# Attention of a two-layer trunk: V of all heads first through DRAM, q and k of a head as one Strassen product

## The chip, the cores and the metric

The kernel runs on one core of one Trainium2 chip. The metric is the device time of one execution in microseconds (us), lower is better. A core has five engines that run their own queues in order and wait for one another by semaphores: TensorE (PE in the profile; its weight loads are PEld), VectorE (DVE), ScalarE (ACT), GpSimd (POOL) and SyncE (SP). SP issues every DMA of this kernel, so a DMA that has to wait for something holds back all DMAs behind it.

## The reference, cut to what matters

One sequence of 1024 tokens with 1024 channels passes two layers: an HGRN2 mixer with its feed-forward network, then dilated attention with a second feed-forward network, and a last norm. The change touches the attention.

```python
def dilated_attention_mixer(u, w_qkv, w_out, cos, sin):        # u: 1 x 1024 x 1024
    qkv = (u @ w_qkv).reshape(B, S, 3, ATTN_HEADS, ATTN_HEAD_DIM)   # 12 heads of 128
    q = apply_rope(qkv[:, :, 0], cos, sin)
    k = apply_rope(qkv[:, :, 1], cos, sin)
    v = qkv[:, :, 2]
    for gi, (window, dilation) in enumerate(((128, 1), (512, 4), (2048, 16))):
        ...                                    # 4 heads each: softmax(mask(q k^T / sqrt(128))) v
        outs.append(o_g); lses.append(lse_g)
    alpha = jax.nn.softmax(lse, axis=2)        # merges the three groups, token by token
    return (o * alpha[..., None]).reshape(B, S, ATTN_WIDTH) @ w_out
```

## The kernel before

Activations lie transposed: a tile has 128 channels as partitions and the 1024 tokens along the row, in two halves of 512 (`hs(hh)`). Each float32 operand of a large product is split into a high and a low part (`split`, `split_w`: ScalarE casts, VectorE subtracts), and a product is three matmuls: high by high, high by low, low by high. The operands `v` of the attention projections are the eight tiles of the normed input, split. `unit` makes one projection of one head: it loads a 512 KB weight tile, splits it, and issues 8 x 2 x 3 matmuls of 128x512 into two PSUM banks (pool `pmm`, four banks).

The loop over j (0 to 3) and gi (0 to 2, dilations 1, 4 and 16) does one head n = 4 gi + j at a time, so heads come in the order 0, 4, 8, 1, 5, 9 and so on. `attn_scores` makes q and k by `unit` and applies the rotary embedding (`rope`), which also writes the tokens in the order of the dilated residue classes (`tok`); for dilations 4 and 16 that is a strided access. Then it makes eight score blocks of 128 rows (tiles `as`, in the four banks of pool `pax`). For each block VectorE adds the mask and takes the row maximum in one instruction into `st` (L671), then scales the maxima (`ng`, L675), and ScalarE takes the exponentials with their sums (L677). `attn_value` makes v of the head, undoes the norm, and transposes it on TensorE (L691). `attn_out` transposes the probabilities (`apx`, L707), copies them back, and multiplies (`apo`, L715). When the three heads of one j have their scores, `attn_weights` sends maxima and sums through DRAM to bring them into token order (`dn`, `cm`), computes the merge weights, and sends these through DRAM (`dw`); `attn_merge` loads each broadcast over partitions (`wb`) and multiplies it into the head's output (L763). After the loop the twelve outputs are split (`aov`), and `mixer_out` multiplies by the output weights (`p_n3..`, two parts of six heads per output tile) and adds the residual. In the second part of a layer, `ffn_in` already uses a two-by-two Strassen form.

The program is recorded in this order, and a scheduler then sets the order of each engine's queue once, before it runs; on the chip each queue is strictly in that order. Buffers come from pools of tags with a fixed number of tiles: `wr` (raw weights) 2, `wh` and `wl` (split weights) 3 each, `wx` 2, `ws` 4, `vc` 8, `va` 16, `vb` 12, each 128 x 1024.

Of the kernel before, what the change touches and what calls it, by code (L numbers as in the profile page):

```python
# [40 lines left out]
def trunk_kernel(ctx, tc, x, cols, consts, w_in, w_hout, w_qkv, w_aout, w_ffn, w_down, out):  # L41
# [588 lines left out]
    def rope(ps, dil, name):  # L630
        t = big("vc", name)
        bb = big("wx", f"{name}b")
        for hh in range(2):
# [4 lines left out]
            nc.vector.tensor_add(tv, tv, nat(bb[:, hs(hh)], dil))
        return t

    def attn_scores(j, gi, st):
# [36 lines left out]
        return blocks, place  # L678

    def attn_value(j, gi):  # L680
        dil = (1, 4, 16)[gi]
# [1 line left out]
        pv = unit(w_qkv[2 * NH + n], v, f"av{n}")
        vt = big("wx", f"avt{n}")
        for hh in range(2):
            nc.vector.tensor_mul(tok(vt, dil, hh), nat(pv[hh][:], dil), nat(rb[:, hs(hh)], dil))
# [208 lines left out]
```

## Time and profile before

| | |
|---|---|
| median of 3 runs | 2608.99 us (2608.29 to 2609.2) |
| span of the profiled execution | 2605.1 us |
| busy, share of the span | PE 98%, PEld 81%, DVE 66%, ACT 30%, POOL 5% |
| attention stage, from the last matmul of the first layer | 1274 us to about 1807 us |

The time of a run is that of the device, some 4 us more than the span from the first to the last instruction of the program. A matmul's end is modelled in the trace, and matmuls overlap, so the work of TensorE is better counted in issue slots than in busy time.

### The profile page before, as it was taken

To read this page: it belongs to the slowest core of one execution; us is meant where nothing else is said; L and a number is where in the kernel's file an instruction comes from. 1 tells how busy PE (TensorE), PEld (TensorE's weight loads), DVE (VectorE), ACT (ScalarE), POOL (GpSimd) and SP (SyncE) were. 2 spreads that over 40 slices of the span, in tenths; PEclk is the share of its full clock that TensorE was granted. 3 is DMA by queue.
4 is the path that set the end of the run, shared out by engine and by line. 5 is a ranking of instruction groups with operands and counts; after the bars stand their busy time and mean duration, and the time that the engine had idled before them with its cause. 6 is when DMAs were issued, how large, how long until landed. Compare 5 with 4: busy or idle time off the path is not lost.

```text
span 2605.1 us, 30351 instructions
## 1 busy us (share of the span) xinstructions
PE 2546.4 (98%) x12044; PEld 2118.4 (81%) x12044; DVE 1732.1 (66%) x2957; ACT 785.1 (30%) x1168; POOL 129.9 (5%) x107
## 2 busy tenths in 40 slices
PE   8999999999999999999999999999999999999998
PEld 6888888788888888888887878787878888888887
DVE  8888888977777777433545464636377777775336
ACT  5222222344323233212231313134242323333212
POOL 1111111111000000000000000000010000000000
PEclk9999999999999999999999999999999999999999
DMA  3101111142222224531211121213322222236323
GB/s 144 33 33 33 33 33 33 44 143 89 79 84 80 89 81 149 183 100 61 97 41 58 41 58 41 61 34 101 115 81 89 81 89 81 81 102 229 110 58 127
DMA packets 77518, 215.24 MB, mean 83 GB/s; under 512 B 21696, under 2 KB 24000, under 8 KB 77376
## 3 DMA queue, kind: packets, MB, share of 16 engines
q1 hardware_dynamic: 77376, 213.30, 25.3%
q8 instruction: 95, 1.56, 0.2%
q14 instruction: 47, 0.39, 0.0%
HBM read 173.28 MB, written 39.99 MB: 82 GB/s over the span
## 4 chain that ended last, share of the span: by engine, by line
PE 81%; DVE 11%; DMA 3%; issue 2%; ACT 1%; POOL 1%; SPq 0%; POOLq 0%; DVEq 0%; ACTq 0%
PE pt L483 6%; PE pt L482 6%; PE pt L481 6%; PE pfw L125 6%; PE pfw L127 6%; PE pfw L124 6%; PE pb L482 4%; PE pb L483 4%; PE pb L481 4%; PE p_n L125 2%; PE p_n L124 2%; PE p_n L127 2%; PE lv L327 2%; PE as L670 1%; PE p_aq L127 1%
## 5 line engine op out<-in xcount | busy, mean ns | idle before, releaser
L563 DVE TENSOR_TENSOR h<-pfw,h 128x512 f32<-128x512 f32 (+1 forms) x104 | 63.6, 646 | 217.6 <-PE pfw L127 217.5
L108 ACT CAST h_fw<-r_fw 128x896 fp32r<-128x896 f32 (+1 forms) x60 | 58.3, 973 | 249.7 <-PE pfw L125 206.4
L108 ACT CAST h_fa<-r_fg 128x1024 fp32r<-128x1024 f32 x44 | 46.4, 1056 | 198.4 <-PE pt L482 183.5
L108 ACT CAST h_fb<-s 128x1024 fp32r<-128x1024 f32 x44 | 46.4, 1054 | 171.1 <-PE pb L482 159.6
L342 DVE COPY_PREDICATED at<-lm,lv 128x192 f32<-128x192 uint8 (+2 forms) x288 | 82.2, 353 | 4.0 <-PE lv L327 3.2
L677 ACT ACTIVATE ap<-ap,ng 128x256 f32<-128x256 f32 (+1 forms) x96 | 41.9, 438 | 124.4 <-DVE ng L675 124.4
L156 POOL TENSOR_TENSOR rs_n<-ms_n,half 128x8 f32<-128x8 f32 (+2 forms) x7 | 9.0, 1281 | 1353.8 <-DVE ms_n L154 1353.8
L494 DVE TENSOR_TENSOR s<-r_fu 128x512 f32<-128x512 f32 x44 | 30.3, 691 | 65.8 <-DMA r_fu<-in_w_ffn_dram 65.7
L482 PE MATMUL pb<-n3b,h_fa 128*128 128x512 f32 x176 | 68.7, 390 | 2.6 <-DVE n3b L456 2.6
L109 DVE TENSOR_TENSOR l_fw<-r_fw,h_fw 128x896 fp32r<-128x896 f32 (+1 forms) x60 | 67.1, 1121 | 4.6 <-ACT h_fw L108 4.0
L482 PE MATMUL pb<-n1b,h_fa 128*128 128x512 f32 x176 | 68.6, 390 | 1.2 <-DVE n1b L456 1.2
L481 PE MATMUL pb<-n3b,h_fa 128*128 128x512 f32 x176 | 68.8, 391 | 0.5 <-ACT n3b L455 0.5
L481 PE MATMUL pt<-n3t,h_fb 128*128 128x512 f32 x176 | 68.6, 390 | 0.0
L481 PE MATMUL pt<-n1t,h_fb 128*128 128x512 f32 x176 | 68.6, 390 | 0.0
L481 PE MATMUL pb<-n1b,h_fa 128*128 128x512 f32 x176 | 68.6, 390 | 0.0
L483 PE MATMUL pb<-n3b,l_fa 128*128 128x512 f32 x176 | 68.5, 389 | 0.0
L482 PE MATMUL pt<-n3t,h_fb 128*128 128x512 f32 x176 | 68.5, 389 | 0.0
L483 PE MATMUL pb<-n1b,l_fa 128*128 128x512 f32 x176 | 68.5, 389 | 0.0
L483 PE MATMUL pt<-n1t,l_fb 128*128 128x512 f32 x176 | 68.5, 389 | 0.0
L483 PE MATMUL pt<-n3t,l_fb 128*128 128x512 f32 x176 | 68.5, 389 | 0.0
L482 PE MATMUL pt<-n1t,h_fb 128*128 128x512 f32 x176 | 68.5, 389 | 0.0
L517 DVE TENSOR_TENSOR t<-pt,t 128x512 f32<-128x512 f32 x44 | 30.4, 691 | 51.0 <-PE pt L483 50.9
(1036 smaller groups left out, 7840.3 us busy)
## 6 DMA issues: line engine op xcount, KB each, us to landing
r_fu<-in_w_ffn_dram SPq DMA_DIRECT2D x44, 512.0 KB, 3.6
r_fg<-in_w_ffn_dram SPq DMA_DIRECT2D x44, 512.0 KB, 3.6
act<-g SPq DMA_DIRECT2D x44, 512.0 KB, 2.6
st<-act SPq DMA_DIRECT2D x44, 512.0 KB, 4.3
r_fw<-in_w_down_dram SPq DMA_DIRECT2D x44, 448.0 KB, 3.4
h<-hd SPq DMA_DIRECT2D x16, 512.0 KB, 5.5
r_fw<-in_w_down_dram SPq DMA_DIRECT2D x16, 512.0 KB, 3.6
r_aq<-in_w_qkv_dram SPq DMA_DIRECT2D x12, 512.0 KB, 3.6
```

Source lines behind the costliest of these rows:

```text
L108: nc.scalar.copy(hi[:, a:b], src[:, a:b])
L109: nc.vector.tensor_sub(lo[:, a:b], src[:, a:b], hi[:, a:b].bitcast(F32))
L124: nc.tensor.matmul(p[:, 0:b - a], wh, vh[:, a:b], start=(first and i == 0), stop=False)
L125: nc.tensor.matmul(p[:, 0:b - a], wh, vl[:, a:b], start=False, stop=False)
L127: nc.tensor.matmul(p[:, 0:b - a], wl, vh[:, a:b], start=False, stop=(last and i == n - 1))
L327: nc.tensor.matmul(ps[:, c * 192:c * 192 + 192], kk[:, hh * 512 + c4 * P:hh * 512 + c4 * P + P], mb[:, c4 * 192:c4 * 192 + 192], start=Tru ...
L342: nc.vector.copy_predicated(av[:, :, d:4, :], mk[:, :, d:4, :], pv[:, :, s0:s0 + 4 - d, :])
L481: nc.tensor.matmul(ps[:], wh, bh, start=(kk == 0), stop=False)
L482: nc.tensor.matmul(ps[:], wh, bl, start=False, stop=False)
L483: nc.tensor.matmul(ps[:], wl, bh, start=False, stop=(kk == 3))
L563: nc.vector.tensor_add(h[d][:, a:b], ps[i][:, 0:b - a], h[d][:, a:b])
L677: nc.scalar.activation(place[b], place[b], AF.Exp, bias=ng[:, b:b + 1], scale=SCALE, accum_out=st[:, gi, b, 1:2])
```

## The change

V is made first, for four heads at once and by tokens: the input is the stationary operand, the weights of four heads (512 columns) are the moving one, and each block of 128 tokens is scaled by the norm, and written to a DRAM tile `vd`. A head later reads its v from there in the order of its dilation, so that no transpose of v is left. The operands are then the blocks b11, b12, b21, b22 of the input, two by two in channels and tokens, and four combinations t1 to t4.

q and k of a head are one product of two-by-two blocks with seven block products instead of eight (`pair`). Each is 12 matmuls; I call them a to g by the weight tiles a to g: a is b11, b is t1, c is t2, d is b21, e is t3, f is b22 and g is t4. Sums are made by accumulating onto a PSUM bank that ScalarE has seeded by a copy: p2 from p1 before c, p3 from p2 before e. q of the first half is ready after d (p1), k of the second after e (p3 and s5), q of the second after f (p2 and s5), and k of the first after g, which accumulates onto p3 once more. `rope` now takes one half at a time: ScalarE copies the two halves of 64 rows into `z`, crossed, VectorE multiplies by sine and cosine and adds. There is one `z` per head, so the four calls of a head follow one another. For the two halves with s5, VectorE first adds s5 in the strided order, and ScalarE then reads that strided tile.

The projections of the next head are recorded ahead of the scores of this one. The probabilities are transposed back into their own tile. Each head's output goes to a DRAM tile `od`, and the merge of all twelve heads (load `am`, load `wb`, multiply, split) stands after the last head.

```diff
@@ -598,25 +598,138 @@
...
+    def halves(w, src, scale=None):
+        hi, lo = w[:, 0:512], w[:, 512:T]
+        if scale is None:
+            nc.scalar.copy(hi, src)
+            nc.vector.tensor_sub(lo, src, hi.bitcast(F32))
+        else:
+            nc.scalar.activation(hi, src, AF.Copy, scale=scale)
+            nc.vector.scalar_tensor_tensor(lo, src, scale, hi.bitcast(F32), ALU.mult, ALU.subtract)
+        return w
 
     def done0(h, d, lo, hi, i):
         nm.add(h[d], d)
         nc.sync.dma_start(hd[1][d], h[d][:])
-        v[d] = split(h[d], "va", f"v2_{d}", gain(2, d))
-
-    ffn_down(0, act0, hd[0], done0)
-    nm.begin()
-    done_ps["aq0"] = unit(w_qkv[0], v, "aq0")
+        for hh in range(2):
+            halves(qops[d % 4][f"b{d // 4 + 1}{hh + 1}"], h[d][:, hs(hh)], gain(2, d))
+
+    h = ffn_down(0, act0, hd[0], done0)
+
+    vd = dp.tile([T, NH * P], F32, name="vd")
+    wn = [0]
+
+    def v_weights(g):
+        ws = []
+        for kp in range(4):
+            raw = big("wr", f"vr{g}_{kp}")
+            for b in range(2):
+                kb = 2 * kp + b
+                src = raw[:, hs(b)]
...
+                w = big(("wh", "wl", "ws")[wn[0] % 3], f"vw{g}_{kb}", F32R)
+                wn[0] += 1
+                ws.append(halves(w, src))
+        return ws
+
+    for g in range(3):
+        ws = v_weights(g)
+        for tt in range(8):
+            ps = mmps(f"pv{g}_{tt}")
+            for kb in range(8):
+                op = qops[kb % 4][f"b{kb // 4 + 1}{tt // 4 + 1}"]
+                o = tt % 4 * P
+                vh, vl = op[:, o:o + P], op[:, 512 + o:512 + o + P]
+                wh, wl = ws[kb][:, 0:512], ws[kb][:, 512:T]
+                nc.tensor.matmul(ps[:], vh, wh, start=(kb == 0), stop=False)
+                nc.tensor.matmul(ps[:], vh, wl, start=False, stop=False)
+                nc.tensor.matmul(ps[:], vl, wh, start=False, stop=(kb == 7))
+            if g == 0 and tt == 0:
+                nm.begin()
+            if tt % 2 == 0:
+                vs = big("wx", f"vs{g}_{tt}")
+            nc.scalar.activation(vs[:, hs(tt % 2)], ps[:], AF.Copy, scale=nm.r[:, tt:tt + 1])
+            nc.sync.dma_start(vd[cs(tt), g * 512:g * 512 + 512], vs[:, hs(tt % 2)])
+
...
+            nc.vector.tensor_sub(dst, x1, x0)
+            qops[kk][n] = halves(big("va" if n == "t4" else "vb", f"q{n}_{kk}", F32R), dst)
+
...
+    def w_half(src, name):
+        wn[0] += 1
+        return halves(big(("wh", "wl")[wn[0] % 2], name, F32R), src)
+
+    def pair_weights(ga, up, name):
+        g0, g1, u0, u1 = ga[:, hs(0)], ga[:, hs(1)], up[:, hs(0)], up[:, hs(1)]
+        w = {"b11": w_half(g0, f"{name}a")}
+        nc.vector.tensor_sub(g0, g0, u0)
+        nc.vector.tensor_add(u0, u0, u1)
+        w["t1"] = w_half(u0, f"{name}b")
+        nc.vector.tensor_sub(u0, u1, g0)
+        w["t2"] = w_half(u0, f"{name}c")
+        w["b21"] = w_half(g1, f"{name}d")
+        nc.vector.tensor_sub(g1, g1, u0)
+        w["t3"] = w_half(g0, f"{name}e")
+        w["b22"] = w_half(g1, f"{name}f")
+        w["t4"] = w_half(u1, f"{name}g")
+        return w
+
+    def seeded(ps, w, ops, n, onto=True):
+        for kk in range(4):
+            wh, wl = w[n][:, cs(kk)], w[n][:, 512 + kk * P:512 + kk * P + P]
+            bh, bl = ops[kk][n][:, 0:512], ops[kk][n][:, 512:T]
+            nc.tensor.matmul(ps[:], wh, bh, start=(kk == 0 and not onto), stop=False, skip_group_check=onto)
+            nc.tensor.matmul(ps[:], wh, bl, start=False, stop=False, skip_group_check=onto)
+            nc.tensor.matmul(ps[:], wl, bh, start=False, stop=(kk == 3), skip_group_check=onto)
+
+    def pair(ga, up, ops, s5, name):
+        w = pair_weights(ga, up, name)
+        p1, p5, p2, p3 = [mmps(f"{n}_{name}") for n in ("p1", "p5", "p2", "p3")]
+        seeded(p1, w, ops, "b11", False)
+        nc.scalar.copy(p2[:], p1[:])
+        seeded(p5, w, ops, "t1", False)
+        nc.scalar.copy(s5, p5[:])
+        seeded(p2, w, ops, "t2")
+        nc.scalar.copy(p3[:], p2[:])
+        seeded(p1, w, ops, "b21")
+        yield p1
+        seeded(p3, w, ops, "t3")
+        yield p3
+        seeded(p2, w, ops, "b22")
+        yield p2
+        seeded(p3, w, ops, "t4")
+        yield p3
...
+    def rope(t, ps, s5, hh, dil, z):
+        tv = tok(t, dil, hh)
+        src, zn = nat(ps[:], dil), nat(z, dil)
+        if s5 is not None:
+            nc.vector.tensor_add(tv, src, nat(s5, dil))
+            src = tv
+        nc.scalar.copy(zn[0:64], src[64:128])
+        nc.scalar.copy(zn[64:128], src[0:64])
+        nc.vector.tensor_mul(z, z, sb[:, hs(hh)])
+        nc.vector.tensor_mul(tv, src, nat(cb[:, hs(hh)], dil))
+        nc.vector.tensor_add(tv, tv, zn)
+
+    def attn_qk(j, gi):
         dil = (1, 4, 16)[gi]
         n = gi * 4 + j
...
+        ga = load_raw(w_qkv[n], D, f"aq{n}")
+        up = load_raw(w_qkv[NH + n], D, f"ak{n}")
+        sz = big("wx", f"sz{n}")
+        s5, z = sz[:, 0:512], sz[:, 512:T]
+        p = pair(ga, up, qops, s5, f"a{n}")
+        q = big("vc", f"aq{n}")
+        k = big("vc", f"ak{n}")
+        rope(q, next(p), None, 0, dil, z)
+        rope(k, next(p), s5, 1, dil, z)
+        rope(q, next(p), s5, 1, dil, z)
+        rope(k, next(p), None, 0, dil, z)
+        return q, k
+
+    def attn_scores(j, gi, st, q, k):
+        n = gi * 4 + j
         blocks = []
...
+    od = dp.tile([NH, P, T], F32, name="od")
+
+    def attn_out(j, gi, vv, blocks, ptiles):
...
+        for ti, (t, where) in enumerate(ptiles):
+            for g1 in range(0, len(where), 4):
+                grp = where[g1:g1 + 4]
+                ps = axps(f"apx{n}_{ti}_{g1}")
+                for c, key in enumerate(grp):
+                    pts[key] = t[:, cs(g1 + c)]
+                    nc.tensor.transpose(ps[:, cs(c)], pts[key], ident)
                 nc.scalar.copy(t[:, g1 * P:(g1 + len(grp)) * P], ps[:, 0:len(grp) * P])
...
-        return o
+        nc.sync.dma_start(od[n], o[:])
...
-    def attn_merge(j, dw, os3):
-        for gi in range(3):
-            wb = big("ws", f"wb{j}_{gi}")
-            nc.sync.dma_start(wb[:], dw[gi].partition_broadcast(P))
-            nc.vector.tensor_mul(os3[gi][:], os3[gi][:], wb[:])
...
+    heads = [(j, gi) for j in range(4) for gi in range(3)]
+    dws = []
+    qk = {heads[0]: attn_qk(*heads[0])}
+    for i, (j, gi) in enumerate(heads):
+        if i + 1 < NH:
+            qk[heads[i + 1]] = attn_qk(*heads[i + 1])
+        if gi == 0:
+            st = sp.tile([P, 3, 8, 2], F32, tag="st", name=f"st{j}", bufs=2)
+        blocks, ptiles = attn_scores(j, gi, st, *qk.pop((j, gi)))
+        if gi == 2:
+            dws.append(attn_weights(j, st))
+        vv = attn_value(j, gi)
+        attn_out(j, gi, vv, blocks, ptiles)
+    ov = []
+    for i, (j, gi) in enumerate(heads):
+        o = big("vc", f"am{j}_{gi}")
+        nc.sync.dma_start(o[:], od[gi * 4 + j])
+        wb = big("wx", f"wb{j}_{gi}")
+        nc.sync.dma_start(wb[:], dws[j][gi].partition_broadcast(P))
+        nc.vector.tensor_mul(o[:], o[:], wb[:])
+        ov.append(split(o, "va" if i < 8 else "vb", f"aov{i}"))
```

How the queues change is seen in three places. Names end in buffer numbers; the digit before it is the head (`ak4` is k of head 4, `as0` a score block of head 0, `a8e` the weights e of head 8, `st0` the statistics of j = 0).

The first is VectorE's queue where a head's rotary embedding meets the scores. Before, k of head 4 is finished and then its own scores are reduced:

```order
L637 TENSOR_TENSOR ak4_10196<-p_ak4_0_10146,cb_9842 128x128x4
L634 TENSOR_TENSOR ak4b_10197<-p_ak4_1_10147,sb_9843 64x512
L638 TENSOR_TENSOR ak4_10196<-ak4_10196,ak4b_10197 128x128x4
L635 TENSOR_TENSOR ak4b_10197<-p_ak4_1_10147,sb_9843 64x512
L637 TENSOR_TENSOR ak4_10196<-p_ak4_1_10147,cb_9842 128x128x4
L109 TENSOR_TENSOR l_ak8_10417<-r_ak8_10414,h_ak8_10416 128x1024
L638 TENSOR_TENSOR ak4_10196<-ak4_10196,ak4b_10197 128x128x4
L671 ISA ap4_0_10206,st0_9848<-as4_1_10209,kon_96 128x256
L671 ISA st0_9848 128x1
L671 ISA ap4_0_10206,st0_9848<-as4_5_10214,kon_96 128x256
```

In the change:

```order
L751 TENSOR_TENSOR sz4_10800<-sz4_10800,sb_10644 128x512
L752 TENSOR_TENSOR ak4_10802<-ak4_10802,cb_10643 128x128x4
L747 TENSOR_TENSOR aq4_10801<-p2_a4_10830,sz4_10800 128x128x4
L753 TENSOR_TENSOR ak4_10802<-ak4_10802,sz4_10800 128x128x4
L612 TENSOR_TENSOR a8e_11043<-r_aq8_11020,a8e_11043 128x512
L799 ISA ap0_0_10942,st0_10941<-as0_1_10945,kon_96 128x256
L799 ISA st0_10941 128x1
L799 ISA ap0_0_10942,st0_10941<-as0_3_10950,kon_96 128x256
L799 ISA st0_10941 128x1
L751 TENSOR_TENSOR sz4_10800<-sz4_10800,sb_10644 128x512
L752 TENSOR_TENSOR aq4_10801<-aq4_10801,cb_10643 128x128x4
L799 ISA ap0_0_10942,st0_10941<-as0_1_10945,kon_96 128x256
```

The reductions of head 0 now stand between the steps of the rotary embedding of head 4, behind an addition that needs p2 of head 4, and the rest of head 4 stands behind them; the scores of head 4 come one head later.

The second is VectorE's queue at the merge weights of a j (`cm` is what comes back from DRAM). Before, for j = 1:

```order
L686 TENSOR_TENSOR avt9_11436<-p_av9_1_11387,rb_n2_9829 128x32x16
L109 TENSOR_TENSOR l_av2_11656<-r_av2_11653,h_av2_11655 128x1024
L741 TENSOR_TENSOR amx1_11365<-cm1_11363 128x8
L742 TENSOR_TENSOR amx1_11365<-amx1_11365,cm1_11363 128x8
L745 TENSOR_TENSOR ae1_11368<-cm1_11363,amx1_11365 128x24
L749 TENSOR_TENSOR ale1_11371<-ae1_11368,cm1_11363 128x24
L751 TENSOR_TENSOR ad1_11373<-ale1_11371 128x8
L752 TENSOR_TENSOR ad1_11373<-ad1_11373,ale1_11371 128x8
L753 RECIPROCAL ad1_11373<-ad1_11373 128x8
L754 TENSOR_TENSOR ae1_11368<-ae1_11368,ad1_11373 128x24
L763 TENSOR_TENSOR ao1_10877<-ao1_10877,wb1_0_11479 128x1024
L634 TENSOR_TENSOR aq2b_11546<-p_aq2_0_11495,sb_9843 64x512
```

In the change, for j = 0:

```order
L803 TENSOR_SCALAR ng8_11383<-st0_10941 128x8
L612 TENSOR_TENSOR a9a_11694<-r_aq9_11687,a9a_11694 128x512
L694 TENSOR_TENSOR r_aq9_11687<-r_aq9_11687,r_ak9_11689 128x512
L695 TENSOR_TENSOR r_ak9_11689<-r_ak9_11689 128x512
L870 TENSOR_TENSOR amx0_11419<-cm0_11417 128x8
L871 TENSOR_TENSOR amx0_11419<-amx0_11419,cm0_11417 128x8
L874 TENSOR_TENSOR ae0_11422<-cm0_11417,amx0_11419 128x24
L612 TENSOR_TENSOR a9b_11699<-r_ak9_11689,a9b_11699 128x512
L878 TENSOR_TENSOR ale0_11425<-ae0_11422,cm0_11417 128x24
L697 TENSOR_TENSOR r_ak9_11689<-r_ak9_11689,r_aq9_11687 128x512
L880 TENSOR_TENSOR ad0_11427<-ale0_11425 128x8
L751 TENSOR_TENSOR sz5_11467<-sz5_11467,sb_10644 128x512
```

The merge itself (L763) is gone from here. The first instruction that reads `cm` now stands ahead of the weights b of head 9 and of the first rotary step of head 5.

The third is SP's queue at the end of the attention. Before, when the last statistics (`dn3`) are sent:

```order
L72 DMA r_n3w4_1_13336<-in_w_aout_dram 128x768
L733 DMA dn3_13053<-st3_12336 512x1x2 x2
L584 DMA n3h0_13233<-hd1_4571 128x1024
L72 DMA r_n3w1_0_13456<-in_w_aout_dram 128x768
L738 DMA cm3_13059<-dn3_13053 128x48
L72 DMA r_fu1_0_14019<-in_w_ffn_dram 128x1024
L72 DMA r_fu1_1_14295<-in_w_ffn_dram 128x1024
L72 DMA r_n3w1_1_13462<-in_w_aout_dram 128x768
L756 DMA dw3_13074<-ae3_13064 128x3x8
L762 DMA wb3_0_13175<-dw3_13074 128x1024
L762 DMA wb3_1_13178<-dw3_13074 128x1024
L762 DMA wb3_2_13181<-dw3_13074 128x1024
```

In the change:

```order
L851 DMA od_10650<-ao7_13202 128x1024
L862 DMA dn3_13267<-st3_12942 512x1x2 x2
L904 DMA am0_0_13319<-od_10650 128x1024
L867 DMA cm3_13273<-dn3_13267 128x48
L851 DMA od_10650<-ao11_13293 128x1024
L904 DMA am0_1_13328<-od_10650 128x1024
L904 DMA am0_2_13337<-od_10650 128x1024
L906 DMA wb0_2_13339<-dw0_11432 128x1024
L904 DMA am1_0_13346<-od_10650 128x1024
L885 DMA dw3_13288<-ae3_13278 128x3x8
L906 DMA wb1_0_13348<-dw1_12099 128x1024
L904 DMA am1_1_13355<-od_10650 128x1024
```

Before, three `wb` loads are left behind the last statistics. Now twelve loads of head outputs and ten of `wb` stand behind them (the two others, for heads 0 and 4, a little ahead), each `wb` into one of two tiles of `wx`; 12 of these 24 rows are shown. On TensorE the transposes of the probabilities of a head now stand between the matmuls c of the head that comes two places later (those of head 0 between `a8c`), and its `apo` matmuls among the matmuls d there.

## Rows read from the trace of the kernel before

**Rows 1.** The page: span, and busy time of each engine.
```profile
span 2605.1 us, 30351 instructions
...
PE 2546.4 (98%) x12044; PEld 2118.4 (81%) x12044; DVE 1732.1 (66%) x2957; ACT 785.1 (30%) x1168; POOL 129.9 (5%) x107
```

**Rows 2.** Windows: stretch, length, busy time (x instructions), clock, DMA share, GB/s.
```profile
640.00:1000.00 360.00, 360.00 (x1590) 298.20 (x1589) 277.70 (x340) 109.64 (x132) 0.00 (x0) 1.00 0.25 84
1274.00:1807.00 533.00, 512.28 (x2546) 423.71 (x2544) 284.71 (x518) 147.10 (x337) 1.64 (x1) 1.00 0.19 54
...
1808.00:1812.00 4.00, 3.35 (x9) 2.62 (x10) 4.00 (x4) 1.95 (x3) 0.00 (x0) 0.64 0.03 8
```

**Rows 3.** The windows of the output projection's matmuls (tile p_n) alone, TensorE.
```profile
1274.00:1807.00 533.00, 19.91 (x83) 1.00 0.19 54
```

**Rows 4.** Waits of TensorE from 1265 to 1830: total, times, longest.
```profile
PE as L670 <- DVE ak L638: 16.5, 11, 1.8
```

**Rows 5.** The chain that ended last: start, us, what.
```profile
1277.70 1.78 PE nm_n L181 x16
...
1304.58 2.31 PE as L670 x10
...
1315.53 1.64 PE apx L707 x15
1317.16 3.35 PE apo L715 x30
```

**Rows 6.** Groups by form: busy us, mean ns | idle before. V's transposes, VectorE.
```profile
L691 PE MATMUL avp<-kon,avt 128*128 128x128 f32 x96 | 14.6, 282 | 2.9 <-DVE avt L686 2.6
...
L671 DVE CUSTOM_DVE_ANT_0 ap<-as,kon 128x256 f32<-128x256 f32 x44 | 18.1, 422 | 4.4 <-PE as L670 3.7
...
L638 DVE TENSOR_TENSOR aq<-aq,aq4b 128x512 f32<-128x512 f32 x2 | 2.2, 1096 | 0.0
...
L638 DVE TENSOR_TENSOR ak<-ak,ak0b 128x512 f32<-128x512 f32 x2 | 1.4, 690 | 0.0
...
L109 DVE TENSOR_TENSOR l_fd<-r_fu,h_fd 128x512 fp32r<-128x512 f32 x19 | 12.9, 681 | 0.0
```

**Rows 7.** The same of ScalarE.
```profile
L677 ACT ACTIVATE ap<-ap,ng 128x256 f32<-128x256 f32 x44 | 21.8, 497 | 89.7 <-DVE ng L675 89.7
L721 ACT COPY ao<-apo 128x512 f32<-128x512 f32 x16 | 16.7, 1070 | 5.9 <-PE apo L715 5.9
...
L717 ACT COPY ao<-apo 128x512 f32<-128x512 f32 x8 | 4.7, 586 | 7.9 <-PE apo L715 7.9
```

**Rows 8.** Timeline of head 9 (dilation 16): VectorE: start, length.
```profile
1503.80 1.08 DVE L637 TENSOR_TENSOR aq<-p_aq,cb 128x512 f32<-128x512 f32 x1
...
1525.28 0.17 DVE L675 TENSOR_SCALAR ng<-st 128x8 f32<-128x8 f32 x1
```

**Rows 9.** Timeline of ScalarE at the exponentials of head 0.
```profile
1309.37 0.49 ACT L677 ACTIVATE ap<-ap,ng 128x256 f32<-128x256 f32 x1
...
1309.86 0.50 ACT L677 ACTIVATE ap<-ap,ng 128x256 f32<-128x256 f32 x1
```

**Rows 10.** Timeline of the last merge, from statistics to output matmuls.
```profile
1787.47 1.21 SPq L733 DMA_DIRECT2D dn<-st  x2
...
1794.05 0.33 SPq L738 DMA_DIRECT2D cm<-dn  x1
...
1797.27 0.17 DVE L741 TENSOR_TENSOR amx<-cm 128x8 f32<-128x8 f32 x1 [2.06 <-DMA cm<-dn]
...
1802.28 1.28 SPq L762 DMA_DIRECT2D wb<-dw  x3
1806.24 2.53 DVE L763 TENSOR_TENSOR ao<-ao,wb 128x1024 f32<-128x1024 f32 x2 [6.51 <-DMA wb<-dw]
...
1808.65 0.83 PE L124 MATMUL p_n<-aov9h,h_n3w 128*128 128x512 f32 x2 [2.63 <-ACT aov9h L144]
```

**Rows 11.** DMA issues: KB each, median us from issue to landing.
```profile
r_aq<-in_w_qkv_dram SPq DMA_DIRECT2D x12, 512.0 KB, 3.6
...
wb<-dw SPq DMA_DIRECT2D x12, 512.0 KB, 4.9
```

**Rows 12.** Timeline of VectorE where the first layer ends.
```profile
1274.33 1.29 DVE L563 TENSOR_TENSOR h<-pfw,h 128x512 f32<-128x512 f32 x2 [4.71 <-PE pfw L127]
```

More of the change, by code (lines that the diff above doesn't have):

```diff
@@ L600, in trunk_kernel @@
     nm = Norm("n2")
-    v = [None] * KT
+    qops = [{n: big("va", f"q{n}_{kk}", F32R) for n in ("b12", "b11")} for kk in range(4)]
+    for kk in range(4):
+        for n in ("b21", "b22"):
+            qops[kk][n] = big("va", f"q{n}_{kk}", F32R)
+    def halves(w, src, scale=None):
[7 more added lines that the diff above has]
+        return w
     def done0(h, d, lo, hi, i):
@@ new lines, in trunk_kernel @@
+    for d in range(KT):
+        nc.scalar.mul(h[d][:], h[d][:], gain(2, d))
+    for n in ("t1", "t3", "t2", "t4"):
+        for kk in range(4):
+            top, bot = h[kk], h[kk + 4]
+            dst, x1, x0 = {
+                "t1": (top[:, hs(0)], top[:, hs(1)], top[:, hs(0)]),
+                "t3": (top[:, hs(1)], bot[:, hs(1)], top[:, hs(1)]),
+                "t2": (bot[:, hs(1)], bot[:, hs(1)], top[:, hs(0)]),
+                "t4": (bot[:, hs(0)], bot[:, hs(0)], bot[:, hs(1)]),
+            }[n]
+            nc.vector.tensor_sub(dst, x1, x0)
+            qops[kk][n] = halves(big("va" if n == "t4" else "vb", f"q{n}_{kk}", F32R), dst)
@@ L677, in attn_scores @@
             nc.scalar.activation(place[b], place[b], AF.Exp, bias=ng[:, b:b + 1], scale=SCALE, accum_out=st[:, gi, b, 1:2])
-        return blocks, place
+        return blocks, ptiles
     def attn_value(j, gi):
+        n = gi * 4 + j
+        vv = big("vc", f"avv{n}")
+        src = vd[:, cs(n)]
+        if gi == 0:
+            nc.sync.dma_start(vv.rearrange("p (c m) -> p c m", m=P), src.rearrange("(c p) m -> p c m", p=P))
+        elif gi == 1:
+            sv = src.rearrange("(i p r) m -> p r i m", p=P, r=4)
+            for r in range(4):
+                nc.sync.dma_start(vv[:, r * 256:r * 256 + 256].rearrange("p (i m) -> p i m", m=P), sv[:, r])
+        else:
+            sv = src.rearrange("(i c r) m -> i r c m", c=8, r=2)
+            for r in range(2):
+                nc.sync.dma_start(vv[r * 64:r * 64 + 64, :].rearrange("p (c m) -> p c m", m=P), sv[:, r])
@@ L681, in attn_value @@
+        return vv
+    od = dp.tile([NH, P, T], F32, name="od")
+    def attn_out(j, gi, vv, blocks, ptiles):
         dil = (1, 4, 16)[gi]
         n = gi * 4 + j
[L683 to L686, printed above, removed]
-        vv = big("vc", f"avv{n}")
-        for hh in range(2):
-            ps = axps(f"avp{n}{hh}")
-            for c in range(4):
-                nc.tensor.transpose(ps[:, cs(c)], vt[:, hh * 512 + c * P:hh * 512 + c * P + P], ident)
-            nc.scalar.copy(vv[:, hs(hh)], ps[:])
@@ L693, in attn_value @@
[L693 to L708 removed]
+        o = big("vc", f"ao{n}")
@@ L757, in attn_weights @@
         return dw
[L759 to L777 removed]
+    heads = [(j, gi) for j in range(4) for gi in range(3)]
[4 more added lines that the diff above has]
+            qk[heads[i + 1]] = attn_qk(*heads[i + 1])
+        if gi == 0:
+            st = sp.tile([P, 3, 8, 2], F32, tag="st", name=f"st{j}", bufs=2)
[12 more added lines that the diff above has]
+        ov.append(split(o, "va" if i < 8 else "vb", f"aov{i}"))
     ops, nm = mixer_out(1, hd[2], hd[1], ov, 2, "n3")
```

53 lines of the change are left out of this document (10 added, 43 removed).

## Prediction, made before the change was run

> **What bounds the kernel now.** I read the page's busy times first: TensorE works 98% of the span, VectorE 66% and ScalarE 30% [rows 1]. The windows then give the change's stretch, the attention stage from 1274 to 1807 us: 533 us, in which VectorE is busy 285 and ScalarE 147 [rows 2]. To count TensorE's work I use slots: in a stretch where it never stops, 1590 matmuls of 512 columns take 360 us, 0.2264 us each [rows 2]. The stage has 36 projections (q, k and v of 12 heads) of 48 matmuls, 1728 slots or 391.2 us. One head of dilation 1 adds 15 score matmuls (10 take 2.31 us), 15 transposes (1.64) and 30 output matmuls (3.35) [rows 5], together 8.5 us. By the same prices dilation 4 (12, 12 and 24) adds 6.9, and dilation 16 (8, 8 and 16) some 4.7; four heads of each make 80.6. The 96 transposes of V take about 10.5 (0.109 each, as the `apx` in [rows 5]; their busy time overlaps, 14.6 in [rows 6]), norm sums 2.6 (`nm_n` in [rows 5], and the like), and 83 matmuls of the output product that fall into the stage 18.8 [rows 3]. That is 503.7, so 29 us of 533 are lost; the largest part is the 16.5 us in which scores wait for the rotary result of their own head [rows 4], and 2.6 are the wait for the last merge [rows 10]. So the stage is TensorE's, and work taken from it counts in full, if VectorE and ScalarE then still come in time.
>
> **What is removed.** Seven block products of 12 matmuls replace eight, so a head's q and k have 84 slots for 96: 144 slots in 12 heads, 32.6 us. V's 96 transposes are another 10.5. V has 576 slots in either form. In all 43.1 us leave TensorE, and 460.6 remain. The merge's multiplies (1.23 us each, from 2.53 for two in [rows 10]) leave the loop for its end.
>
> **What is added in the loop.** I follow a period, from the end of product d of one head to the end of d of the next, for dilation 4. The four calls of `rope` share one `z`, so their copies, multiplies and additions form one chain. Prices: a contiguous ScalarE copy 0.586, a strided one 1.07 [rows 7]; a VectorE operation of 128x512 0.69 contiguous, 1.10 strided [rows 6], 1.08 from PSUM [rows 8]. No row has ScalarE reading a strided tile, which two of the four calls now do; 64 rows of 512 cost no less than 0.586 and, by the strided write, 1.07. I take the upper end, since the stride is the same, and keep the lower. I add 0.2 for each hand-over between engines (an estimate, from the 0.17 that the smallest instruction takes [rows 8]).
>
> Call the end of d zero. q of the first half: two copies 1.17, hand-over 0.2, then 0.69, 1.08 and 1.10, so 4.3. Its neighbour's addition p3+s5 ends at 5.3; this matters because g overwrites p3, and TensorE has f until 5.44 (24 slots). k of the second half: copies 2.14, 0.2, then 0.69, 1.08, 1.10 and, queued between, the second s5 addition, with which it ends near 11.0. q of the second half starts its copies when `z` is free: 2.14, 0.2, 2.9 make 16.1. k of the first half takes 4.1 as the first did: 20.2. The reductions of the head before (0.42 each with 256 columns [rows 6]) stand between these steps. Those left over and `ng` (0.17 [rows 8]) bring it to 21.1. Only then come the eight exponentials, 0.49 apart [rows 9]: 25.1. Their transposes stand inside product c of the next head, which therefore ends at about 25.9, and d with the outputs between (2.72 and 3.35) at 31.9. TensorE's own work in the period is 84 slots and 8.5 us, 27.5. So 4.5 us are lost. In a period of dilation 16 the chain is as long, its end shorter by 0.65 (24 outputs instead of 30, dilation 4's), and TensorE's own work 25.9: 31.3, 5.4 lost. In one of dilation 1 all is contiguous: `ng` at 15.4, last exponential 18.5, d ends at 23.6 against TensorE's 23.7: nothing lost. Load is not the limit: counting the instructions of a period at these prices, VectorE has some 23 us of work, ScalarE some 18.
>
> The period of heads 5, 6 and 7 has one thing more. The first reader of `cm` stands on VectorE ahead of their first rotary step, and behind it are queued that head's whole chain and a weight split. The statistics are complete at 18.5 of the period before. From the issue of `dn` to the first result out of `cm` the last merge took 9.8 us [rows 10] (1787.47 to 1797.27). At 28 `cm` is in, while that period's d ended at 23.6; with the small operations on it the chain starts some 4.8 late. p3+s5 then ends near 10.4, g waits 5 us for it, and the period takes 36.0: 8.6 lost, three times. Sum of the loop: 4.5, 3 x 8.6 and 3 x 5.4 (the last head has no successor): **46.5 us**.
>
> [...]
>
> **What is added at the end.** After the last g (call it T) nothing is left to hide behind. The chain of head 11 runs on 12 us, `ng` of head 7 comes at T+14, its exponentials end at T+17.5; transposes, copies and outputs of head 7, then reductions and exponentials of head 11 take some 8.5 more, to X = T+26. Then SP, in order: `dn3`, and behind it `cm3`, issued 6.6 us after `dn` [rows 10] because it waits for it, and behind that `am` and `wb` of nearly all heads. The first multiplies come near X+12 (`am` lands some 4 us after its issue, by `r_aq` of the same 512 KB [rows 11]). `wb` has two tiles, so a `wb` waits for the multiply two before it: issue 0.35, landing 4.9 [rows 11] or 4.0 (6.24 less 2.24, alone, [rows 10], 1802.28 to 1806.24), multiply 1.23, some 5.5 for two heads. Five such rounds, 27.5, put the last multiply at X+41, and its split at X+44. Of these 70 us TensorE has work for 28 (6.9 and 4.7 of the last two heads, 72 slots of the output product). Lost: **42 us**, where before 2.6 were lost [rows 10]. The bounds: 15, if the transfers are early enough that only the chain to X counts, and 50.
>
> **What is added at the start.** V's blocks of 128 tokens need all channels at once, so the first one waits for the last two results of the layer before: additions of 0.65 (1.29 for two, [rows 12]), norm sums, casts and splits, some 6 us against 4.8 us of matmuls ahead of them. I take 1.5. The next groups' weights come through the two tiles `wr`, and I take 2 us at each of two borders: **6 us** in all, bounds 0 and 12. The four combinations t1 to t4 (16 subtractions of 0.68 and 16 splits, [rows 6]) have all of V's 130 us beside them and cost nothing; without that cover they would be 22 us.
>
> **The sum.** 460.6 + 46.5 + 42 + 6 = 555.1 against 533: 22 us more. The profiled span of 2605.1 becomes 2627. The median of the runs is 3.9 above the span, which gives **2631 us**. Differences under 0.2% (5 us) can't be told from no change.
>
> **Rivals.** (1) *The loop is hidden.* If the next head's products do cover ropes and scores, as recorded, the loop loses 10 or less. For it: the 16.5 us of [rows 4] were a wait for a rotary result with nothing between, and now a whole product set lies between; VectorE and ScalarE have spare time in sum. Against it: the chain of 25 us above, in which they wait for each other. Then -43.1 and 10 + 42 + 6 less the 29 lost before: 16 us less and up to 30 less, 2589 (2575 to 2600). This one ends on the other side; it decides where the chain from d to the last exponential is below some 21 us in the strided periods. (2) *Loop and end are both hidden*, the end losing 15: 2560. (3) *ScalarE reads strided tiles at full speed and `cm` comes in time.* That takes 13 us (1.9 in each of 7 periods) and 13 more (4.1 in each of 3): 2605 (2600 to 2614), about no change. [...]
>
> [...]
>
> **How the numbers follow.** The forecast (2613 to 2645): 0.55. Rival 1: 0.18; 2: 0.06; 3: 0.13; 4: 0.08. Faster: rivals 1 and 2, a third of 3, 0.28; same: most of 3 and the lower edge of the forecast, 0.12; slower 0.60. The range leaves out rival 2, the lowest part of 1 and the upper half of 4: 2578 to 2655. The forecast's own range is 2613 to 2645.
>
> **What would show it.** Right: waits of TensorE for ScalarE (probabilities) inside c in the periods of dilation 4 and 16, and before g for VectorE's p3+s5 in heads 5 to 7; VectorE idle on the transfer `cm` ahead of them; period lengths of 32, 36, 31 and 24 us; some 70 us from the last g to the last merged head with TensorE mostly idle, waiting for `aov`, VectorE for `wb`; V's part 130 us and about 6. Wrong: periods near 27 us (rival 1); ScalarE's copies out of strided tiles at 0.6 us each (rival 3); a clock below 1 all through the loop (rival 4); a short end, or V's part with long gaps.

## The result and the profile after

The changed kernel takes 2624.93 us (2623.98 to 2626.84) against 2608.64 of before beside it: ratio 1.0064, interval 1.005 to 1.0078, so 0.64% slower. The forecast was 2631 us.

The page after:

```profile
span 2622.2 us, 30501 instructions
PE 2528.1 (96%) x11804; PEld 2091.0 (80%) x11804; DVE 1764.8 (67%) x3069; ACT 923.2 (35%) x1400; POOL 130.0 (5%) x107
```

TensorE is busy 18 us less than in [rows 1] in a span 17 us longer: it waits for work. The windows tell where (the columns are those of [rows 2]: stretch, length, then busy time of TensorE's matmuls, its weight loads, VectorE, ScalarE and GpSimd, then clock, DMA share and GB/s):

```profile
1274.00:1408.00 134.00, 134.00 (x600) 111.20 (x599) 28.63 (x48) 36.02 (x58) 2.02 (x1) 1.00 0.29 93
1451.00:1484.00 33.00, 28.79 (x149) 23.45 (x148) 22.47 (x44) 20.76 (x42) 0.00 (x0) 1.00 0.21 65
1516.00:1542.00 26.00, 25.02 (x126) 19.70 (x125) 18.31 (x49) 17.65 (x39) 0.00 (x0) 1.00 0.30 83
1542.00:1574.00 32.00, 28.03 (x144) 22.42 (x143) 21.23 (x42) 18.80 (x40) 0.00 (x0) 1.00 0.22 67
1756.00:1797.00 41.00, 22.53 (x94) 16.51 (x92) 15.50 (x49) 18.52 (x47) 0.00 (x0) 0.68 0.31 86
1797.00:1824.00 27.00, 23.97 (x84) 15.92 (x85) 20.11 (x22) 9.03 (x11) 0.00 (x0) 0.92 0.91 319
```

V's part (first row) has no gap. In the loop's stretches with strided heads TensorE is busy some 87%, and VectorE and ScalarE about two thirds: over a whole period none of the three is full. The 41 us behind the last g hold 94 matmuls, at a mean clock of 0.68. Of the waits of TensorE in the stage, those from 0.9 us on (total, times, longest):

```profile
PE as L798 <- DVE st L799: 34.9, 25, 4.6
PE p_a L710 <- DVE ak L747: 6.7, 5, 3.0
PE apx L837 <- ACT ap L805: 5.7, 5, 1.2
PE p_n L124 <- ACT aov0h L144: 5.0, 1, 5.0
PE p_n L125 <- DVE aov6l L145: 1.1, 1, 1.1
PE apo L844 <- ACT ap L838: 0.9, 1, 0.9
```

The scores no longer wait for their own rotary result (16.5 in [rows 4]). They wait for a PSUM bank: a head's score blocks, its transposes and its outputs take turns in the four banks of `pax`, and the reductions that free the banks stand between the rotary steps of the next head. Of the 34.9 us, 24.9 lie in the loop and 10.0 behind the last g.

The start of product e, which ends a period, shows the period lengths (TensorE's timeline):

```profile
1507.63 0.39 PE L710 MATMUL p_a<-qt,a1e 128*128 128x512 f32 x1
...
1532.41 0.39 PE L710 MATMUL p_a<-qt,a5e 128*128 128x512 f32 x1
...
1565.81 0.39 PE L710 MATMUL p_a<-qt,a9e 128*128 128x512 f32 x1
...
1598.33 0.39 PE L710 MATMUL p_a<-qt,a2e 128*128 128x512 f32 x1
```

The rotary calls of head 1 (dilation 1) have 24.8 us, those of head 5 (dilation 4) 33.4, of head 9 (dilation 16) 32.5. Inside head 5's period, VectorE and ScalarE:

```profile
1532.66 0.17 DVE L870 TENSOR_TENSOR amx<-cm 128x8 f32<-128x8 f32 x1
...
1537.74 1.02 DVE L747 TENSOR_TENSOR ak<-p_a,sz 128x512 f32<-128x512 f32 x1
...
1543.33 1.04 DVE L753 TENSOR_TENSOR ak<-ak,sz 128x512 f32<-128x512 f32 x1
1544.28 0.42 DVE L799 CUSTOM_DVE_ANT_0 ap<-as,kon 128x256 f32<-128x256 f32 x1
...
1548.62 1.05 DVE L753 TENSOR_TENSOR aq<-aq,sz 128x512 f32<-128x512 f32 x1
...
1552.71 1.06 DVE L753 TENSOR_TENSOR ak<-ak,sz 128x512 f32<-128x512 f32 x1
1553.68 0.16 DVE L803 TENSOR_SCALAR ng<-st 128x8 f32<-128x8 f32 x1
```

```profile
1538.85 1.14 ACT L749 COPY sz<-ak 64x512 f32<-64x512 f32 x1 [2.83 <-DVE ak L747]
1540.02 1.12 ACT L750 COPY sz<-ak 64x512 f32<-64x512 f32 x1
...
1544.46 1.08 ACT L749 COPY sz<-aq 64x512 f32<-64x512 f32 x1 [0.34 <-DVE ak L753]
...
1557.34 0.39 ACT L805 ACTIVATE ap<-ap,ng 128x128 f32<-128x128 f32 x1
```

Counted from the end of d (1532.41), the steps that the forecast gave for a plain period of dilation 4 as 5.3, 11.0, 16.1, 20.2, 21.1 and 25.1 end at 6.3, 12.0, 17.3, 21.4, 21.4 and 25.3: the chain is there, step by step, up to about 1 us late. (Head 5 is one of the three heads for which the forecast had set a delay by `cm` on top.)

### The profile page after: what moved, and what is told of

Its sections match the earlier page's. It is cut to its first block, busy times and chain, and to the rows that moved or that the text cites. A ratio compares the mean times of both kernels' runs of the same rounds, so it can differ in the third digit from the quotient of the medians.

```text
span 2622.2 us, 30501 instructions
## 1 busy us (share of the span) xinstructions
PE 2528.1 (96%) x11804; PEld 2091.0 (80%) x11804; DVE 1764.8 (67%) x3069; ACT 923.2 (35%) x1400; POOL 130.0 (5%) x107
## 4 chain that ended last, share of the span: by engine, by line
PE 79%; DVE 12%; ACT 4%; DMA 2%; issue 2%; POOL 1%; SPq 0%; POOLq 0%; DVEq 0%; ACTq 0%
PE pt L483 6%; PE pt L481 6%; PE pt L482 6%; PE pfw L125 6%; PE pfw L127 6%; PE pfw L124 6%; PE pb L482 4%; PE pb L483 4%; PE pb L481 4%; PE p_n L125 2%; PE p_n L127 2%; PE p_n L124 2%; PE pv L654 2%; PE pv L656 2%; PE pv L655 2%
## 5 line engine op out<-in xcount | busy, mean ns | idle before, releaser
L798 PE MATMUL as<-ak,aq 128*128 128x256 f32 (+1 forms) x192 | 44.8, 355 | 35.1 <-DVE st L799 34.9
L655 PE MATMUL pv<-vw,qb 128*128 128x512 f32 x192 | 74.9, 390 | 0.0
L654 PE MATMUL pv<-vw,qb 128*128 128x512 f32 x192 | 74.9, 390 | 0.0
L656 PE MATMUL pv<-vw,qb 128*128 128x512 f32 x192 | 74.8, 390 | 0.0
L798 PEld LDWEIGHTS as<-ak,aq 128*128 128x128 f32 x192 | 32.6, 197 | 51.3 <-DVE st L799 48.1
L483 PE MATMUL pb<-n3b,l_fa 128*128 128x512 f32 x176 | 68.8, 391 | 0.0
L481 PE MATMUL pt<-n1t,h_fb 128*128 128x512 f32 x176 | 68.7, 390 | 0.0
```

Source lines behind the costliest of these rows:

```text
L481: nc.tensor.matmul(ps[:], wh, bh, start=(kk == 0), stop=False)
L483: nc.tensor.matmul(ps[:], wl, bh, start=False, stop=(kk == 3))
L654: nc.tensor.matmul(ps[:], vh, wh, start=(kb == 0), stop=False)
L655: nc.tensor.matmul(ps[:], vh, wl, start=False, stop=False)
L656: nc.tensor.matmul(ps[:], vl, wh, start=False, stop=(kb == 7))
L798: nc.tensor.matmul(ps, q[:, cs(b)], k[:, ks[0] * P:ks[0] * P + w], start=True, stop=True)
```

## The experiments

Each experiment ran in five rounds beside the kernel before.

| | us | ratio to before, interval |
|---|---|---|
| change | 2624.9 | 1.0064 (1.005 to 1.0078) |
| e1_natural_s5 | 2601.5 | 0.9968 (0.9956 to 0.998) |
| e2_natural_two_z | 2600.6 | 0.9966 (0.9953 to 0.9978) |
| e3_early_merge | 2614.4 | 1.0021 (1.0012 to 1.003) |
| e4_eight_products | 2607.2 | 0.999 (0.9982 to 0.9999) |
| e5_natural_early | 2590.8 | 0.993 (0.9917 to 0.9943) |
| e6_eight_early | 2588.3 | 0.9922 (0.9909 to 0.9935) |
| e7_tensor_strided | 2599.0 | 0.9963 (0.9949 to 0.9977) |
| e8_no_lookahead | 2651.2 | 1.0159 (1.0143 to 1.0175) |
| e9_tensor_strided_early | 2585.7 | 0.9911 (0.9897 to 0.9925) |
| e10_hybrid_early | 2587.1 | 0.9915 (0.9902 to 0.9929) |

**The chain's strided half heads.** e1 (`c` is the natural order in runs, `n` the same element by element; `acc` is for k the half of its own tile that is written last, for q the tile of s5 itself):

```diff
+        nc.vector.tensor_add(c(acc), c(ps[:]), c(s5))
+        nc.scalar.copy(c(z)[0:64], c(acc)[64:128])
...
+        nc.vector.tensor_add(tok(t, dil, 1).rearrange("p (a i) r -> p a i r", a=dil), n(acc), n(z))
```

> Edit: in dilations 4 and 16 the two half heads with s5 get that sum in natural order (VectorE writes runs of 128 or 32 columns), ScalarE copies from it in natural order, and only the last addition writes with a stride. Nothing is left out. Theory (the loop's loss is the length of the chain from product d through the four rotary calls to the exponentials): each such half is shorter by 0.35 (sum), 1.0 (two copies 0.6 instead of 1.1) and 0.36 (product with the cosine), so a strided head by some 3.4 us; the seven strided periods of 32.5 to 35.5 us become some 29 to 31, sum about -24, 2600 us (2595 to 2608). Rival (VectorE's load, or the score banks that wait for its reductions whatever the chain): only VectorE's own saving counts, 1.4 us a head, -10, 2615. Rival (the exponentials or the transposes bound the period): no change, 2625.

Measured: 23.4 us less than the change (forecast 24). On VectorE, ScalarE and TensorE: the sum now takes 0.68 instead of 1.02, a copy 0.62 instead of 1.14, and head 5's period 31.0 instead of 33.4, while head 1's is still 24.8:

```profile
1534.55 0.68 DVE L754 TENSOR_TENSOR ak<-p_a,sz 128x512 f32<-128x512 f32 x1
```

```profile
1535.32 0.62 ACT L755 COPY sz<-ak 64x512 f32<-64x512 f32 x1 [2.53 <-DVE ak L754]
```

```profile
1528.96 0.39 PE L710 MATMUL p_a<-qt,a5e 128*128 128x512 f32 x1
...
1559.95 0.39 PE L710 MATMUL p_a<-qt,a9e 128*128 128x512 f32 x1
```

The waits of scores for `st` fall from 34.9 to 15.2 us. That speaks for the chain; by VectorE's load alone 10 us were due. In head 9's period `ng` comes 3.4 us sooner (19.0 for 22.4 us behind the end of d), of which 1.6 are less work on VectorE and 1.8 less waiting of it.

**The one `z`.** e2 is e1 with

```diff
-            rope5(k, next(p), s5, runs(k, dil, 0), dil, z)
+            rope5(k, next(p), s5, runs(k, dil, 0), dil, runs(q, dil, 1))
```

> As e1, and the second rotary call of a strided head (k, second half) has a scratch of its own (the half of q's tile that is not yet written) in place of the one z. Nothing is left out. Theory of the chain: the third call's copies need no longer wait for the second call's last addition, 2 to 3 us less in each of seven periods beyond e1: strided periods near 28, 2588 us (2580 to 2596). Rival (load or score banks): the same as e1, within 5 us.

Measured: the same as e1; the theory's 12 us more were not there. The third call's copies did start earlier, but the fourth's still wait for VectorE to finish the third (2.48 us, "ACT sz L767 <- DVE aq L759"), and VectorE takes all in one order. It has no room to use an earlier copy in head 5's period: from the end of d to `ng` it is busy 18.0 of 18.7 us (18.4 of 19.0 in e1). So a second scratch for one call gains nothing, and there the chain is VectorE's queue, with ScalarE's copies in it. That the shared scratch costs nothing at all is not shown: the third and fourth calls of e2 still share `z`, and the addition that the fourth waits for reads it.

**Eight products.** e4 leaves out the form of the change; each half of q or k is 24 matmuls, over two blocks of channels (`b`), into one bank:

```diff
-        rope(k, next(p), s5, 1, dil, z)
-        rope(q, next(p), s5, 1, dil, z)
+        rope(q, next(p), None, 1, dil, s5)
...
+                for b in range(2):
```

> q and k of a head with eight block products instead of seven (no seeds, no s5, no t1 to t4, z in the two halves of the same tile in turn); V first, the look-ahead and the merge at the end stay. Nothing of the result is left out. Theory of the chain: TensorE gets 32.6 us more work, but the rotary calls read PSUM in natural order, do not wait for a sum with s5, and start half a product set apart, so that the chain hides and the loop loses some 10 us instead of 50: 2625 + 32.6 - 40, about 2618 us (2610 to 2628). Rival (the loss comes from VectorE's load or from the scores' banks): the periods are longer by the 2.7 us of the twelve matmuls, 2650 (2640 to 2658).

Measured: 2607.2, 18 us less than with seven products and below the theory's range, although TensorE has 144 slots (32.6 us) more. From the first matmul of q and k to the last g (e4; the change):

```profile
1409.50:1745.50 336.00, 334.00 (x1675) 276.19 (x1674) 177.11 (x383) 154.10 (x358) 0.00 (x0) 1.00 0.28 77
```

```profile
1409.00:1756.00 347.00, 311.54 (x1529) 249.65 (x1528) 239.02 (x486) 208.13 (x430) 0.00 (x0) 0.99 0.26 74
```

VectorE has 177 us of work there instead of 239, ScalarE 154 instead of 208. The loop is nearly covered: 336 us against 329.6 of slots, with 2.0 us of waits in it. The other 7 us are at the end, where the chain of the last head is shorter (33.6 us from the last matmul of q and k to the first output product, after 41). The edit takes away the sums with s5, the seeds and the single `z` together, so it does not say which of them made the loss.

**The end.** e3:

```diff
-        o = big("vc", f"am{j}_{gi}")
+        o = big("vb", f"am{j}_{gi}")
...
-        wb = big("wx", f"wb{j}_{gi}")
+        wb = big("vb", f"wb{j}_{gi}")
```

> The merge's tiles am and wb come from the pool vb (12 tiles, free once the last head's operands t1 to t3 are used) in place of vc and wx; by this the loads of the first nine heads stand ahead of the last statistics on SP, and output products stand among the scores and transposes of head 11. Nothing is left out. Theory (38 us are lost behind the last g because the output product has nothing to start on before 1797): the output product starts some 15 us earlier and fills the waits, -15 to -20, 2608 us (2602 to 2615). Rival (the loads of 9 MB contend with the loads of V and the statistics, or the waits of head 11 only move): -5 or less, 2620 to 2626.

Measured: 10.5 us less, where 15 to 20 were expected. Output products now stand among the score matmuls of head 11, but only behind the outputs of head 7; the scheduler set none into the 23 us ahead of those, in which TensorE is busy 13. What remains behind them is a 4.9 us wait for the last heads.

e5 asks if the gains add:

> e1 and e3 together (natural-order sums with s5, early merge). Nothing is left out. If the loop's loss and the end's are separate, their gains add: 2625 - 23 - 10.5, 2591 us (2587 to 2596). Rival: the early merge gains by filling the waits of head 11's own chain, which e1 has already shortened, so that the two overlap: 2596 to 2602.

They do: 2590.8, 10.7 less than e1. With eight products:

> e4 and e3 together (eight products, early merge). Nothing is left out. Gains add: 2607 - 10.5, 2597 us (2592 to 2601). With it V first, the look-ahead and the transposes of the probabilities stand alone against the kernel before; theory: they are worth the 10.5 us of V's transposes and most of the 16.5 us of score waits, less what the end costs, about -12 against before. Rival: all that the look-ahead gains is lost again at the end, no difference from before, 2607.

Measured: 2588.3, 19 less than e4 and below the expected range. This is 21 us less than the kernel before, with eight products: most of what the best versions gain does not need the seven. Here t1 to t4 don't exist, and output products stand already among the scores of head 7 (probably because the tiles of `vb` are free sooner; no run tests that). The stretch from the last matmul of q and k on in the windows, and all of TensorE's waits in the stage from 0.5 us on:

```profile
1752.00:1795.00 43.00, 36.72 (x201) 30.14 (x199) 18.21 (x55) 18.80 (x49) 0.00 (x0) 0.99 0.44 129
```

```profile
PE as L770 <- DVE st L771: 8.1, 10, 2.3
PE p_n L124 <- ACT aov9h L144: 4.9, 1, 4.9
```

**Where the stride is paid.** e7 (the first line is that of the rotary calls):

```diff
-        dil = (1, 4, 16)[gi]
+        dil = 1
...
-            nc.tensor.matmul(ps, q[:, cs(b)], k[:, ks[0] * P:ks[0] * P + w], start=True, stop=True)
+                nc.tensor.matmul(
+                    ps[c:c + m, :], dilated(q, dil, b * P + c, m), dilated(k, dil, ks[0] * P, w), start=True, stop=True
+                )
```

> All rotary calls work in natural token order (as for dilation 1); TensorE reads q and k with a stride of 4 or 16 floats in the score matmuls (dilation 16: two of 64 rows for each of 128). Seven products, merge at the end. Nothing is left out. Theory of the chain: all periods behave as those of dilation 1 (24.8 against 23.7), loss about 1.5 us each: the loop loses some 15 instead of 50, the end 5 less, 2587 us (2580 to 2595). Rival (a strided operand slows TensorE: the score matmuls take twice as long or more): +3 to +10 in the scores, 2595 to 2605. Rival (not the stride, but the order of VectorE's queue holds the period): as e2, 2600.

(`dilated` picks the tokens of a residue class; in dilation 16 each score matmul becomes two of m = 64 rows.) Measured 2599.0: the chain vanishes (score waits 4.0 us in all), but TensorE pays for the stride: the same ten score matmuls of a head of dilation 4 (as the trace counts them) take 4.28 us, and in e4 (second row), from contiguous tiles, 2.25:

```profile
1562.79 4.28 PE L808 MATMUL as<-ak,aq 128*128 128x256 f32 x10
```

```profile
1483.98 2.25 PE L770 MATMUL as<-ak,aq 128*128 128x256 f32 x10
```

The first rival held. By its time alone e7 could be the second rival's 2600 as well; the score waits rule that out. The period in which the scores of dilation 16 stand (the one with the rotary calls of dilation 1) is 27.4 instead of 24.8; how much of this is the stride and how much the double number of matmuls, no run separates. With the early merge:

> e7 and e3 together. Nothing is left out. If the gains are separate: 2599 - 10.5, 2588.5 us (2584 to 2593). Rival: since in e7 the chain behind the last g is already short, the early merge finds its heads sooner and the wait for head 11 shrinks as well, as it did with eight products (19 instead of 10.5): 2578 to 2583.

Measured 2585.7, inside the first expectation, and the lowest time found: 0.89% below the kernel before. Its interval overlaps those of e6 and e10. A mixture of e2 and e9:

> e9, but dilation 16 writes q and k in dilated order again, with natural-order sums and the second scratch as in e2 (so its score matmuls are contiguous and 8 instead of 16), and only dilation 4 is read with a stride by TensorE. Nothing is left out. By the periods of e2 and e7 (28.5 to 29 for the rotary calls of dilation 16 plus 1.8 for the strided scores of dilation 4, 29.0, and 24.8 instead of 27.4) the loop loses 1 us less for each three heads: within 5 us of e9. Rival (the chain of dilation 16 shows again in full): 5 to 10 us more than e9.

Measured 2587.1, no difference from e9.

**The look-ahead.** e8:

```diff
-        if i + 1 < NH:
-            qk[heads[i + 1]] = attn_qk(*heads[i + 1])
+        qk[heads[i]] = attn_qk(*heads[i])
```

> The changed kernel with the recording order of before: the scores of a head are recorded behind its own projections and ahead of the next head's (the scheduler still puts three products of the next head in front of them). Nothing is left out. Theory of the chain: from the last g the chain runs on some 12 us in the strided heads, three products cover 8 of it, so the scores wait 4 to 6 us in eight heads and the exponentials follow in the next two products; about the same loss as with the look-ahead, 2615 to 2640. Rival (the look-ahead hides most of the chain as it is): some 12 us more in each of eight strided heads, 2680 or more.

Measured 2651.2, between the two: 26 us slower than with the look-ahead. The scores wait for their own rotary result, once a head:

```profile
PE as L798 <- DVE ak L753: 63.6, 12, 12.7
```

So the look-ahead hides 26 us net. With eight products it hides all but 2.0 us of the waits (e4); the longer chain of the seven products it can't hide.

## Why the prediction was right, and where its terms were off

The sum of the forecast against the trace (slots of [rows 2] and the prices of [rows 5], as there):

| term | forecast | measured |
|---|---|---|
| TensorE's work | 460.6 | 460.6 |
| lost at the start | 6 | 1.8 |
| lost in the loop | 46.5 | 50.3 |
| lost at the end | 42 | 37.7 |
| stage | 555.1 | 550.4 |

The measured losses: V's first matmul is at 1275.61 instead of 1274 and q's first at 1408.82, 133.2 us for 576 slots and the norm sums; from there to the first score behind the last g, 1756.11, are 347.3 us for 1008 slots (228.2) and ten heads' scores (68.8); and the 83rd output matmul, with which the stage of before ended, is at about 1824, 68.1 us for 11.6 and 18.8 of work. 550.4 against 533 are 17.4; the spans differ by 17.1. The forecast then set the median 3.9 us above the span, and it is 2.7 above (2624.93 for 2622.2): 3.9 was the difference of a median and of another execution's span, while one execution's time is some 1.8 above its own span (2623.98 for 2622.2). Some slips in the working do not reach the result: by its own prices the heads of dilation 4 and 16 add 6.8 and 4.5 us, not 6.9 and 4.7, which moves 1.6 us from work to loss on both sides of the table, and rival 1's terms make 14 us less, not 16.

**Loop, size nearly right, in part by luck.** The chain had the forecast length (above), but not the forecast make-up. The forecast let VectorE wait out ScalarE's copies, and said that load is not the limit. In head 5's period VectorE is busy 20.0 of the 21.4 us from the end of d to `ng`, with weight splits and reductions beside the copies, and waits for the copies 1.0 us (4.1 of 22.4 in head 9's). It is nearly full in the stretch that counts and has little to do only behind it (third busy time of each row):

```profile
1532.41:1553.84 21.43, 17.47 (x75) 13.35 (x73) 20.01 (x47) 10.99 (x16) 0.00 (x0) 1.00 0.17 50
1553.84:1565.81 11.97, 11.27 (x72) 9.67 (x73) 4.66 (x8) 8.95 (x26) 0.00 (x0) 1.00 0.35 109
```

The forecast's 46.5 us were waits alone. Of the 50.3 the trace names 35 as waits (24.9 of the scores, 6.7 before g, 3.3 for probabilities); the rest lies in slots longer than the prices (some 3 us of it by the clock, below) and behind the modelled ends of matmuls (0.39 us each, 0.23 apart), which hide a part of each wait. In head 1's period TensorE waits 0.2 us and still takes 24.8 us for 23.7 of work. That the two sums come out so near is in part luck.

The step that failed is "From the issue of `dn` to the first result out of `cm` the last merge took 9.8 us": in the loop it takes 5.5 to 6.1 (1527.13 to 1532.66 for j = 0), and VectorE hardly waits for it (0.5 us at most); g is held 0.8 to 1.4 us in heads 5 to 7, not 5. On SP's queue:

```profile
1527.13 1.23 SPq L862 DMA_DIRECT2D dn<-st  x2
1530.68 0.33 SPq L867 DMA_DIRECT2D cm<-dn  x1
```

The forecast took the price from the last merge only. Those three periods are 33.4 to 33.9 instead of 36.0. In exchange the others are longer: dilation 16 32.5 (31.3), dilation 1 24.8 (23.7), and head 4 35.5 (31.9), where the raw weights of head 8 landed late: VectorE waits for them ahead of the rotary steps (1.84 us on the transfer `r_ak`), ScalarE's copies stand behind that split, and g waits 3.0 us. These errors nearly cancelled. Missed as well was the place of the wait: the forecast let TensorE run into product c and wait there for exponentials; it stops earlier, at the score blocks, whose four banks are held by the late reductions.

**Single `z`.** The forecast named it as what makes the chain. e2 lifted it for one of the four calls, and nothing was gained; VectorE's busy times above say why. No run lifts it for all four.

**ScalarE's strided reads.** The upper bound was right: 1.06 to 1.14 us each, with a stride of 256 or 64 elements, so rival 3 fell. e1 bears out the price of the stride (0.62 without it). A stride of only four elements was paid for as well: by TensorE's score matmuls of dilation 4 in e7 (4.28 against 2.25 us), and by ScalarE's writes of the outputs of dilation 4 in the kernel before (1.08 to 1.09 us in heads 4 to 7, 0.586 contiguous [rows 7]).

**End, size nearly right.** The exponentials of head 11 end at 1788.34, 32 us behind the last g (forecast 26). The statement that five rounds of `wb` through two tiles set the pace was wrong: VectorE's order does, which multiplies a head, waits for ScalarE's cast of it, splits it, and only then takes the next head, 3.48 us each (VectorE's timeline):

```profile
1803.22 1.22 DVE L907 TENSOR_TENSOR am<-am,wb 128x1024 f32<-128x1024 f32 x1
1805.55 1.23 DVE L145 TENSOR_TENSOR aov2l<-am,aov2h 128x1024 fp32r<-128x1024 f32 x1 [1.12 <-ACT aov2h L144]
1806.69 1.22 DVE L907 TENSOR_TENSOR am<-am,wb 128x1024 f32<-128x1024 f32 x1
```

That pace was nearly covered, since the output product took the heads as they came. What cost was the 41 us ahead of it.

**Rival 4, the clock.** That the granted clock falls behind TensorE's long waits came true at the end, and hardly in the loop. The 20 to 30 us that the forecast set for this rival, and with them the 2655 us at the upper edge of its wider range, rest on such a fall behind each of ten long waits of the loop and on more at the end; no run shows that loss. In the loop the clock fell twice, each time behind a score wait of 2.7 us (in the periods of heads 8 and 9), and not behind the equal wait in head 10's:

```profile
1488.00:1492.00 4.00, 4.00 (x12) 3.18 (x12) 3.00 (x5) 1.59 (x2) 0.00 (x0) 0.63 0.00 0
1580.00:1584.00 4.00, 4.00 (x14) 3.07 (x13) 3.91 (x10) 1.40 (x3) 0.00 (x0) 0.61 0.00 0
1670.00:1678.00 8.00, 5.75 (x27) 4.14 (x25) 6.98 (x16) 3.72 (x6) 0.00 (x0) 1.00 0.21 60
```

From the missing shares of the clock in the first two rows that is some 3 us in all, an estimate. Behind the last g the granted clock was 0.68 over 41 us, of which TensorE was busy 22.5. The 24 output matmuls of head 7 took 5.12 us there, at a clock of 0.55, those of head 6 2.84 in the loop, at 1.00 (TensorE's timeline):

```profile
1684.74 2.84 PE L844 MATMUL apo<-ap,avv 128*128 128x128 f32 x24
...
1776.45 5.12 PE L844 MATMUL apo<-ap,avv 128*128 128x128 f32 x24 [0.95 <-ACT ap L838]
```

In e6, where TensorE has output products to do in that place, the clock there was 0.99. How much of the 37.7 us the clock alone took, no run separates.

**Start.** V's part hides its weights through two tiles `wr`; the 4 us set for two borders did not occur.

## What to carry to other kernels

A saving on the busiest engine counts only where the others can still feed it: seven products for eight saved 33 us of TensorE's slots and lengthened the chain of VectorE and ScalarE, so that eight were 18 us faster until the chain was cut. With the chain cut seven were 6 us faster (e1 against e4), and with the early merge as well 2.6 us (e9 against e6), which the intervals do not tell from nothing. An engine that is two thirds busy over a period can be full in the one stretch that the next product waits for, so look at its busy time there (VectorE in head 5's period: 20.0 of 21.4 us). Write a sum that is read twice in the order in which it is contiguous, and let only the last write be strided (e1: 0.68 instead of 1.02 us for the sum, 0.62 instead of 1.14 for a copy). When work is collected at the end of a stage, give it buffers that are free before the end, so that the next stage's products can fill the waits of the last item (e3: 10.5 us less).
